# Expert weights in one run per partition, and fetched rows turned by 64x64 products

## The chip, the cores and the metric

One core of a Trainium2 chip runs the kernel alone. The metric is the device time of one execution in microseconds (us); the number that counts is the median of several executions.

## What is computed

The kernel is one encoder layer on 1024 tokens of 1024 channels with 16 meta tokens in front: a mixer (long convolutions and a gated recurrence), then a mixture of experts, then a norm. The change lies in the mixture of experts. Each token picks one of 8 groups and in it two of 8 experts, so two of 64 experts in all:

```python
def expert_block(args):
    xe, e = args
    return (jax.nn.silu(xe @ w_gate[e]) * (xe @ w_up[e])) @ w_down[e]
```

`w_gate[e]` and `w_up[e]` are 1024 x 512, `w_down[e]` is 512 x 1024, all float32, so each matrix has 2 MB and all 64 experts' matrices 403 MB. The outputs of a token's two experts are weighted and added to the residual.

## The kernel before

All 64 experts run one after the other, each on 64 slots for tokens (1024 tokens with two experts each fill 32 of 64 on average; slots beyond 64 of an expert are the business of `overflow`, behind a branch). The mixer and the router come first and end some 870 us after the start; they aren't touched by the change.

**Loads.** `expert_weights` (lines 1285 to 1306) loads one matrix, in the order gate, up, down of expert 0, then of expert 1, and so on, all on SP's queue. There are nine buffers, three experts' worth. Two things hold a load back: its buffer must have been used, and the load two before it must have landed (`AHEAD = 2`, a dependency that is added by hand), so that two loads are under way at any time. The first seven have their places early; the eighth and ninth (w_up and w_down of expert 2) wait for the rows of the first experts to be fetched. A matrix lies in SBUF as 128 partitions of 16 KB. Of w_down, partition p takes four rows of the matrix, which lie behind each other in memory: one run of 16 KB. Of w_gate and w_up, partition p takes rows 4p to 4p + 3 of the upper half of the matrix and the same of the lower half: two runs of 8 KB. The last w_up of all is loaded in two pieces of 1 MB, each with an instruction of its own, and only the second counts for the depth of the queue.

**Rows.** `fetch` gathers an expert's 64 rows of tokens by an indirect DMA from POOL: partition 64 h + s gets half h (512 channels and the norm's factor) of the row in slot s. Five buffers hold fetched rows. Slots without a token are left out of the transfer.

**One expert** (`expert`, lines 1321 to 1351). TensorE turns the rows: four transposes of 128x128 bring channels to partitions (`xt`), VectorE multiplies by the norm's gain into SBUF. Then sixteen products, alternating between w_gate and w_up, give `gu` in one PSUM bank, gate in partitions 0 to 63 and up in 64 to 127 (two column tiles of 64). ScalarE scales it into SBUF, four transposes (`ht`) turn it, ScalarE and VectorE apply silu and the product, and eight products with w_down give `y`. VectorE copies it out, and an indirect DMA from POOL scatters it to `yd` in DRAM. The `xt` tile in PSUM has one bank, in SBUF two buffers, so the rows of an expert are turned three experts ahead of their use.

**Order.** Each engine works in the order that a scheduler put down when the kernel was built; no table was written by hand. In the trace one product in float32 shows as two records of TensorE (and two weight loads), a transpose as one.

**After the experts**, `final` reads `yd`, adds, normalises and writes the output; it can begin when the last scatter has landed.

```python
    for j in range(4):
        nc.tensor.transpose(pt[:, j].rearrange("p h s -> p (h s)"), xg[:, j:512:4], e.ident)
...
    for i in range(8):
        h, j = divmod(i, 4)
        for z, w in enumerate((wg, wu)):
            nc.tensor.matmul(pg[64 * z:64 * z + 64], xt[:, j, h], w[:, h, j], start=i == 0, stop=i == 7)
```

## Time and profile before

| | |
|---|---|
| time, median of 3 runs | 1903.22 us (1899.13, 1903.22, 1906.44) |
| span of the profiled execution, first to last instruction | 1901.4 us |
| time of the profiled execution | not listed apart from the three runs; its span is 1.8 us below their median |
| mean granted TensorE clock, as a share of full speed | 0.963 |
| TensorE busy | 1627.3 us (86%) |
| TensorE weight loads | 979.9 us (52%) |
| VectorE, ScalarE, GpSimd busy | 817.9, 462.5, 184.5 us |
| moved by DMA | 574.54 MB, mean 302 GB/s |
| DMA busy, share of the 16 engines, in the 40 slices | 0.2 to 0.8 up to slice 17, then 0.9 or more to slice 38 |

The table has shares of the whole span, and the kernel has two parts with different limits. The experts fill slices 18 to 39 of the 40 (47.5 us each); what a change in them is worth must be read from those slices, from the waits of SP's queue and of TensorE there. A matmul's busy time runs to a modelled end and overlaps with that of its neighbours, so starts are a better guide than durations where many small products follow each other.

### The profile page before, as it was taken

The page shows a single profiled execution, that of the slowest core. Times are in us where ns is not written, and L with a number is a line of the kernel's source. Part 1 is how long each engine was busy: PE and PEld are TensorE (multiplying, and loading weights), DVE is VectorE, ACT ScalarE, POOL GpSimd, SP SyncE. Part 2 cuts the span into 40 slices and gives each one's busy share as a digit, 9 for nine tenths or more (in the row PEclk, how much of TensorE's full clock was granted, in tenths as well). Part 3 has the DMA queues.
Part 4 walks back from the last instruction along what each step waited for, and adds up shares of the span by engine and source line. Part 5 has one row for each costly group of instructions (what it writes and reads, how often), then busy time and mean ns, then how long its engine had stood idle before and what let it go on. Part 6 is the DMA issues. An engine that isn't in the chain of part 4 may idle for free. (4 is left out here: it accounts for less than half of the span.)

```text
span 1901.4 us, 22984 instructions
## 1 busy us (share of the span) xinstructions
PE 1627.3 (86%) x8907; PEld 979.9 (52%) x8907; DVE 817.9 (43%) x1661; ACT 462.5 (24%) x879; POOL 184.5 (10%) x223
## 2 busy tenths in 40 slices
PE   5999999999999798997998888888888888888882
PEld 3988988788787576883332223232222222222221
DVE  7678879687787987772111111111111111111106
ACT  5443345253436643331000000000000000000002
POOL 0011100000000001002111111111111111111000
PEclk7999999999999898998999999999999999999996
DMA  5365776566636437278999999999999999999987
GB/s 166 97 213 182 231 217 193 173 213 203 186 115 223 156 103 172 89 305 329 419 418 419 411 416 409 416 417 421 420 417 416 410 419 419 398 416 420 419 342 278
DMA packets 166887, 574.54 MB, mean 302 GB/s; under 512 B 20531, under 2 KB 85135, under 8 KB 125752
## 3 DMA queue, kind: packets, MB, share of 16 engines
q1 hardware_dynamic: 139816, 511.82, 68.6%
q0 software_dynamic: 25808, 57.00, 10.1%
q10 hardware_dynamic: 1152, 4.23, 0.5%
q8 instruction: 71, 1.16, 0.2%
q14 instruction: 40, 0.33, 0.1%
HBM read 532.79 MB, written 57.02 MB: 310 GB/s over the span
## 5 line engine op out<-in xcount | busy, mean ns | idle before, releaser
L1334 PE MATMUL gu<-w,xt 128*64 128x512 f32 x2048 | 517.1, 603 | 83.6 <-DMA w<-in_w_up 82.8
L1334 PEld LDWEIGHTS gu<-w,xt 128*64 128x64 f32 x2048 | 158.8, 138 | 425.8 <-issue 294.4
L1329 DVE TENSOR_TENSOR xt<-xt,gain 128x512 f32<-128x512 f32 x64 | 44.3, 692 | 535.0 <-PE gu L1334 497.0
L1347 PE MATMUL y<-w,ht 128*64 128x512 f32 x1024 | 238.3, 605 | 27.7 <-DVE ht L1342 27.7
L1336 ACT ACTIVATE gu<-gu,xg 128x512 f32<-128x512 f32 x64 | 44.0, 687 | 861.9 <-PE gu L1334 861.9
L480 PE MATMUL w<-al,wh 128*128 128x346 f32 (+2 forms) x672 | 235.1, 350 | 0.0
L480 PE MATMUL w<-ah,wh 128*128 128x346 f32 (+2 forms) x672 | 234.0, 349 | 0.7 <-ACT ah L232 0.7
L480 PE MATMUL w<-ah,wl 128*128 128x346 f32 (+2 forms) x672 | 233.6, 350 | 0.0
L1349 DVE COPY y<-y 128x512 f32<-128x512 f32 x64 | 44.3, 692 | 245.2 <-PE y L1347 245.2
L1347 PEld LDWEIGHTS y<-w,ht 128*64 128x64 f32 x1024 | 69.6, 138 | 153.9 <-issue 112.2
L480 PEld LDWEIGHTS w<-ah,wh 128*128 128x128 f32 x672 | 128.8, 192 | 10.9 <-issue 1.5
L480 PEld LDWEIGHTS w<-ah,wl 128*128 128x128 f32 x672 | 128.7, 192 | 10.8 <-issue 2.0
L480 PEld LDWEIGHTS w<-al,wh 128*128 128x128 f32 x672 | 128.8, 192 | 10.6 <-issue 1.6
L1315 POOL DMA_INDIRECT xg<-rdr,src x64 | 64.8, 1012 | 493.3 <-ACT gu L1336 483.5
L1350 POOL DMA_INDIRECT yd<-y,dst x64 | 64.9, 1014 | 374.7 <-DVE y L1349 374.7
L1339 PE MATMUL ht<-ident,gu 128*128 128x128 f32 x256 | 47.7, 309 | 49.9 <-ACT gu L1336 49.8
L1339 PEld LDWEIGHTS ht<-ident,gu 128*128 128x128 f32 x256 | 35.6, 208 | 102.8 <-ACT gu L1336 102.8
L1342 DVE TENSOR_TENSOR ht<-ht 128x256 f32<-128x256 f32 x64 | 26.9, 421 | 94.5 <-ACT ht L1341 92.5
L482 ACT ACTIVATE pc<-w 128x346 f32<-128x346 f32 (+2 forms) x84 | 41.8, 498 | 73.9 <-PE w L480 68.6
L470 ACT CAST wh<-w 128x512 fp32r<-128x512 f32 x64 | 39.6, 620 | 63.1 <-PE w L480 55.1
L446 PE MATMUL h<-fh,ftab 128*128 128x256 f32 x256 | 52.7, 287 | 2.2 <-ACT fh L433 2.0
L1327 PE MATMUL xt<-ident,xg 128*128 128x128 f32 x256 | 42.9, 290 | 11.4 <-DMA xg<-rdr,src 10.4
(421 smaller groups left out, 2255.4 us busy)
## 6 DMA issues: line engine op xcount, KB each, us to landing
w<-in_w_gate SPq DMA_DIRECT2D x64, 2048.0 KB
w<-in_w_down SPq DMA_DIRECT2D x64, 2048.0 KB
w<-in_w_up SPq DMA_DIRECT2D x63, 2048.0 KB
w<-in_w_in SPq DMA_DIRECT2D x64, 256.0 KB
ftab<-in_tab POOLq DMA_DIRECT2D x32, 384.0 KB, 4.2
tb<-in_tabf POOLq DMA_DIRECT2D x16, 768.0 KB, 6.1
ti<-in_tabi POOLq DMA_DIRECT2D x16, 640.0 KB, 5.4
kdr<-V SPq DMA_DIRECT2D x16, 512.0 KB
```

What stands on the lines that cost most here:

```text
L446: nc.tensor.matmul(A[-1][:, z * HC:z * HC + HC], lhs, rhs, start=i == 0, stop=i == len(prods) - 1)
L480: nc.tensor.matmul(pt[:, :n], lhs[k // 4][:, k % 4, :], rhs[:, k, c0:c0 + n], start=i == 0, stop=i == 3 * KT - 1)
L482: nc.scalar.activation(dst[:, c0:c0 + n], pt[:, :n], func)
L1315: d = nc.gpsimd.indirect_dma_start(out=xg, out_offset=None, in_=rows, in_offset=bass.IndirectOffsetOnAxis(ap=src, axis=0), bounds_check=2 ...
L1327: nc.tensor.transpose(pt[:, j].rearrange("p h s -> p (h s)"), xg[:, j:512:4], e.ident)
L1329: nc.vector.tensor_mul(xt, pt, gain[:, :, :, None].to_broadcast([P, 4, 2, SLOTS]))
L1334: nc.tensor.matmul(pg[64 * z:64 * z + 64], xt[:, j, h], w[:, h, j], start=i == 0, stop=i == 7)
L1336: nc.scalar.activation(gu, pg, AF.Copy, scale=xg[:, 512:513])
L1339: nc.tensor.transpose(pu[:, j].rearrange("p h s -> p (h s)"), gu[:, j::4], e.ident)
L1347: nc.tensor.matmul(py[64 * z:64 * z + 64], ht[:, j], wdv[:, j, z], start=j == 0, stop=j == 3)
L1349: nc.vector.tensor_copy(y, py)
L1350: nc.gpsimd.indirect_dma_start(out=ydv, out_offset=bass.IndirectOffsetOnAxis(ap=dst, axis=0), in_=y, in_offset=None, bounds_check=4 * SEQ ...
```

## The change

w_gate and w_up are laid out so that partition p takes rows 8p to 8p + 7 of the matrix: one run of 16 KB. Channel 8p + j then belongs to partition p. A row's half h holds channels 512 h to 512 h + 511, that is partitions 64 h to 64 h + 63, so the turned rows of half h must come out on these 64 partitions. The four 128x128 transposes become sixteen products of 64x64 (8 values of j, 2 halves) with the identity, at tile position (0, 0) for the first half and (64, 64) for the second. The turned tile has the same 512 columns as before, and the sixteen products with the weights stay as they were. The last w_up loses its two pieces and comes whole, as all others. All three matrices are loaded by one statement (line 1299 in the new file). The gain of the norm is loaded in the new layout. The comments are gone and lines move by one or two.

```diff
 def expert_weights(e, pools, i, after=None):
-    w = pools[i % 9].tile([P, 2, 4, 512], F32, name="w")
-    if j < 2:
-        src = I[("w_gate", "w_up")[j]][0, x].rearrange("(h p j) f -> p h j f", h=2, j=4)
-        if i == 3 * NE - 2:
-            nc.sync.dma_start(w[:, 0], src[:, 0])
-            d = nc.sync.dma_start(w[:, 1], src[:, 1])
-        else:
-            d = nc.sync.dma_start(w, src)
-    else:
-        d = nc.sync.dma_start(w.rearrange("p h j f -> p (h j f)"), I["w_down"][0, x].rearrange("(p j) c -> p (j c)", j=4))
+    w = pools[i % 9].tile([P, 8, 512], F32, name="w")
+    d = nc.sync.dma_start(w, weight_rows(I, ("w_gate", "w_up", "w_down")[j], x))
...
+def weight_rows(I, name, x):
+    m = I[name][0, x]
+    if name == "w_down":
+        return m.rearrange("(p j) (z c) -> p (j z) c", j=4, z=2)
+    return m.rearrange("(p j) f -> p j f", j=8)
...
 def expert(e, ps, xp, W, xg, dst, gain, ydv):
-    pt = ps.tile([P, 4, 2, SLOTS], F32, name="xt")
-    for j in range(4):
-        nc.tensor.transpose(pt[:, j].rearrange("p h s -> p (h s)"), xg[:, j:512:4], e.ident)
+    pt = ps.tile([P, 8, SLOTS], F32, name="xt")
+    for j in range(8):
+        for h in range(2):
+            r = slice(64 * h, 64 * h + 64)
+            nc.tensor.matmul(pt[r, j], xg[r, j:512:8], e.ident[r, r], start=True, stop=True, tile_position=(64 * h, 64 * h))
...
-            nc.tensor.matmul(pg[64 * z:64 * z + 64], xt[:, j, h], w[:, h, j], start=i == 0, stop=i == 7)
+            nc.tensor.matmul(pg[64 * z:64 * z + 64], xt[:, j], w[:, j], start=j == 0, stop=j == 7)
```

The scheduler puts the new products elsewhere than the transposes stood. This is TensorE's order for one expert x in the middle of the program, before; `gu` and `y` are the products with the weights, `ht` the transposes behind `gu`, and `xt` belongs to expert x + 3:

```order
L1334 MATMUL gu<-w,xt 64x512 x16
L1339 MATMUL ht<-ident,gu 128x128 x4
L1327 MATMUL xt<-ident,xg 128x128 x4
L1347 MATMUL y<-w,ht 64x512 x8
L1334 MATMUL gu<-w,xt 64x512 x16
```

The same place of the changed kernel:

```order
L1336 MATMUL gu<-w,xt 64x512 x15
L1341 MATMUL ht<-ident,gu 128x128 x4
L1330 MATMUL xt<-ident,xg 64x64 x14
L1348 MATMUL y<-w,ht 64x512 x8
L1336 MATMUL gu<-w,xt 64x512
L1330 MATMUL xt<-ident,xg 64x64 x2
L1336 MATMUL gu<-w,xt 64x512 x15
```

Fourteen of the sixteen new products stand where the four transposes stood, between `ht` and `y`; the last two have moved behind the next expert's first product with w_gate, ahead of its first product with w_up. The order is the same for all experts from about the tenth to the last that has rows to turn; in the first ten, eleven of the sixteen stand ahead of `ht`.

This is SP's queue at the last loads of weights, before:

```order
L1298 DMA w<-in_w_down 128x4096
L1296 DMA w<-in_w_gate 128x2x2048
L1293 DMA w<-in_w_up 128x2048
L1294 DMA w<-in_w_up 128x2048
L1298 DMA w<-in_w_down 128x4096
```

And of the changed kernel:

```order
L1299 DMA w<-in_w_down 128x4096
L1299 DMA w<-in_w_gate 128x4096
L1299 DMA w<-in_w_up 128x4096
L1299 DMA w<-in_w_down 128x4096
```

Every load of weights is now 128 pieces of 4096 numbers, where w_gate and w_up were 128 times two pieces of 2048, and the two half loads of the last w_up are one.

## Rows read from the trace of the kernel before

**Rows 1.** The page: span; DMA busy in 40 slices; GB/s in the same.

```profile
span 1901.4 us, 22984 instructions
...
DMA  5365776566636437278999999999999999999987
GB/s 166 97 213 182 231 217 193 173 213 203 186 115 223 156 103 172 89 305 329 419 418 419 411 416 409 416 417 421 420 417 416 410 419 419 398 416 420 419 342 278
```

**Rows 2.** Waits of SP's queue: total us, times, longest.

```profile
SPq L1296 <- DMA w<-in_w_up: 319.7, 63, 7.8
SPq L1298 <- DMA w<-in_w_gate: 292.2, 62, 8.9
SPq L1296 <- DMA w<-in_w_down: 287.7, 60, 5.7
```

**Rows 3.** Waits of all engines: TensorE's for weights.

```profile
PE gu L1334 <- DMA w<-in_w_up: 82.8, 49, 3.2
```

**Rows 4.** Timeline of SP's queue, three stretches: start us, us, issue.

```profile
1180.31 0.37 SPq L1296 DMA_DIRECT2D w<-in_w_gate  x1
1185.24 0.37 SPq L1296 DMA_DIRECT2D w<-in_w_up  x1
...
1300.90 0.34 SPq L1298 DMA_DIRECT2D w<-in_w_down  x1
...
1316.45 0.34 SPq L1298 DMA_DIRECT2D w<-in_w_down  x1
...
1795.51 0.37 SPq L1296 DMA_DIRECT2D w<-in_w_gate  x1
1800.77 0.37 SPq L1296 DMA_DIRECT2D w<-in_w_up  x1
1805.72 0.34 SPq L1298 DMA_DIRECT2D w<-in_w_down  x1
1810.69 0.37 SPq L1296 DMA_DIRECT2D w<-in_w_gate  x1
...
1825.85 0.37 SPq L1296 DMA_DIRECT2D w<-in_w_gate  x1
1826.27 0.46 SPq L1293 DMA_DIRECT2D w<-in_w_up  x1
1830.70 0.34 SPq L1294 DMA_DIRECT2D w<-in_w_up  x1
1836.05 0.33 SPq L1298 DMA_DIRECT2D w<-in_w_down  x1
```

**Rows 5.** Timeline of TensorE for one expert in the middle.

```profile
1314.14 0.75 PE L1339 MATMUL ht<-ident,gu 128*128 128x128 f32 x4 [0.83 <-ACT gu L1336]
...
1314.72 0.64 PE L1327 MATMUL xt<-ident,xg 128*128 128x128 f32 x4
...
1315.82 3.65 PE L1347 MATMUL y<-w,ht 128*64 128x512 f32 x16 [0.45 <-DVE ht L1342]
...
1319.30 1.02 PE L1334 MATMUL gu<-w,xt 128*64 128x512 f32 x2
...
1321.77 7.08 PE L1334 MATMUL gu<-w,xt 128*64 128x512 f32 x30 [1.45 <-DMA w<-in_w_up]
```

**Rows 6.** Timeline of TensorE in the recurrence: small float32 products in column tiles.

```profile
619.12 0.46 PE L936 MATMUL b<-lf,s 128*32 128x32 f32 x32
...
623.97 0.20 PE L936 MATMUL f<-qnb,s 128*32 128x32 f32 x1
624.10 0.27 PE L936 MATMUL f<-qff,kff 128*64 128x64 f32 x1
...
624.21 0.22 PE L936 MATMUL f<-qff,kff 128*64 128x64 f32 x1
```

**Rows 7.** Waits of SP's queue, 860 to 905 us.

```profile
SPq L1296 <- PE gu L1334: 1.4, 1, 1.4
```

**Rows 8.** Timeline of TensorE, the last expert.

```profile
1838.89 7.04 PE L1334 MATMUL gu<-w,xt 128*64 128x512 f32 x32
```

More of the change, by code (lines that the diff above doesn't have):

```diff
@@ L1324, in expert @@
     wg, wu, wd = W
-    pt = ps.tile([P, 4, 2, SLOTS], F32, name="xt")
-    for j in range(4):
-        nc.tensor.transpose(pt[:, j].rearrange("p h s -> p (h s)"), xg[:, j:512:4], e.ident)
-    xt = xp.tile([P, 4, 2, SLOTS], F32, name="xt")
-    nc.vector.tensor_mul(xt, pt, gain[:, :, :, None].to_broadcast([P, 4, 2, SLOTS]))
+    pt = ps.tile([P, 8, SLOTS], F32, name="xt")
[3 more added lines that the diff above has]
+            nc.tensor.matmul(pt[r, j], xg[r, j:512:8], e.ident[r, r], start=True, stop=True, tile_position=(64 * h, 64 * h))
+    xt = xp.tile([P, 8, SLOTS], F32, name="xt")
+    nc.vector.tensor_mul(xt, pt, gain[:, :, None].to_broadcast([P, 8, SLOTS]))
     pg = ps.tile([P, 512], F32, name="gu")
-    for i in range(8):
-        h, j = divmod(i, 4)
+    for j in range(8):
         for z, w in enumerate((wg, wu)):
-            nc.tensor.matmul(pg[64 * z:64 * z + 64], xt[:, j, h], w[:, h, j], start=i == 0, stop=i == 7)
+            nc.tensor.matmul(pg[64 * z:64 * z + 64], xt[:, j], w[:, j], start=j == 0, stop=j == 7)
     gu = xp.tile([P, 512], F32, name="gu")
@@ L1342, in expert @@
     nc.vector.tensor_mul(ht, ht, pu[:, :, 1])
-    wdv = wd.rearrange("p h j f -> p (h j f)").rearrange("p (j z c) -> p j z c", j=4, z=2)
     py = ps.tile([P, 512], F32, name="y")
@@ L1346, in expert @@
         for z in range(2):
-            nc.tensor.matmul(py[64 * z:64 * z + 64], ht[:, j], wdv[:, j, z], start=j == 0, stop=j == 3)
+            nc.tensor.matmul(py[64 * z:64 * z + 64], ht[:, j], wd[:, 2 * j + z], start=j == 0, stop=j == 3)
     y = xp.tile([P, 512], F32, name="y", bufs=3)
@@ L1423, in overflow @@
             for j, name in enumerate(("w_gate", "w_up", "w_down")):
-                w = op.tile([P, 2, 4, 512], F32, name=f"ow{j}")
+                w = op.tile([P, 8, 512], F32, name=f"ow{j}")
                 src = I[name][0, bass.ds(x, 1)].rearrange("e a b -> (e a) b")
                 if j < 2:
-                    nc.sync.dma_start(w, src.rearrange("(h p j) f -> p h j f", h=2, j=4))
+                    src = src.rearrange("(p j) f -> p j f", j=8)
                 else:
-                    nc.sync.dma_start(w.rearrange("p h j f -> p (h j f)"), src.rearrange("(p j) c -> p (j c)", j=4))
+                    src = src.rearrange("(p j) (z c) -> p (j z) c", j=4, z=2)
+                nc.sync.dma_start(w, src)
                 W.append(w)
@@ L1668, in build @@
         last = [w_out_load(e, wc, (6, 7), cs, f"l{i}") for i, cs in enumerate(columns(512))]
-        gain = kp.tile([P, 2, 4], F32, name="gain")
-        nc.sync.dma_start(gain, I["norm_ffn"].rearrange("o (h p j) -> p (o h) j", h=2, j=4))
-        gain = gain.rearrange("p h j -> p j h")
+        gain = kp.tile([P, 8], F32, name="gain")
+        nc.sync.dma_start(gain, I["norm_ffn"].rearrange("o (p j) -> (o p) j", j=8))
         for tt in range(8):
```

## The prediction

> **What bounds the kernel now.** I read the page first, and in it the slices. From slice 18 on the DMA engines are busy at 0.9 or more and move 398 to 421 GB/s, and before it they are far from that [rows 1]. So the experts' part is the place, and what counts there is how fast the weights come. The waits of SP's queue say the same from the other side: nearly every load is issued at the moment when the load two before it lands, 319.7 + 292.2 + 287.7 us of waiting on loads in all [rows 2]. The reader is to see that the queue never waits for a buffer: loads wait for loads. TensorE then waits for what comes late, w_up, 82.8 us in 49 times, 1.29 us for each of the 64 experts [rows 3].
>
> Because a load is issued when the one two before it lands, the times of issue in SP's timeline are times of landing, and the distance of two of them is what one load took of the engines' time. One expert goes from 1300.90 to 1316.45, so 15.55 us for three matrices [rows 4]. TensorE's timeline of the same expert shows the slack: behind the first product with w_gate (1319.30) it waits until 1321.77, and 1.45 us of that is the wait for w_up [rows 5]. So the loads set the pace, and TensorE is about a tenth faster.
>
> **The change, part by part.**
>
> *The runs of 16 KB.* The trace already holds loads with such runs: w_down. In the last experts no rows are fetched any more and the landings are clean. From the issue of w_up at 1800.77 to that of w_down at 1805.72 landed a w_gate: 4.95 us. From there to 1810.69 landed a w_up: 4.97 us. From 1795.51 to 1800.77 landed a w_down, 5.26 us, but with the scatter of an expert's output among it. A w_down without that stands elsewhere: 1180.31 to 1185.24, 4.93 us [rows 4]. So 2 MB in runs of 16 KB take 4.93 us and in runs of 8 KB 4.95 to 4.97 us; the gain is 0.02 us for a w_gate and 0.04 for a w_up, and I take 0.02 for each. 123 loads of w_gate and w_up lie on the path: those of experts 3 to 63 and the w_up of expert 2, which is the first that waits for the rows. The term is 123 x 0.02 = 2.5 us less. Its bounds: nothing at all, if 0.02 is chance; and the shortest w_down that I find, from 1825.85 to 1830.70, 4.85 us [rows 4], which is 0.10 below a w_gate, so 12.3 us less. I take the 4.93, since the 4.85 comes from the place where the half loads disturb the queue. A loss I exclude, since w_down has been loaded in just this way all along.
>
> *The last w_up.* It came in halves, the first issued at 1826.27 right behind the last w_gate and ahead of its turn, the second at 1830.70. Thanks to that, the last expert's sixteen products began at 1838.89, as soon as TensorE was free, and ended 7.04 us later at 1845.93 [rows 4, 8]. Now w_up is issued whole at 1830.70. The last w_gate lands at 1836.05 (that is when the last w_down was issued), and w_up lands 4.97 us later, at 1841.02. From there the remaining products take 7.08 us, as they do for any other expert that waits for w_up [rows 5], so they end at 1848.10: 2.2 us more. Behind them lies the chain to the last scatter, and then the final norm, with nothing beside it; this term is on the path in full. The last w_down lands 4.93 us behind w_up, at 1845.95, before those products end, and holds nothing up.
>
> *Sixteen products for four transposes.* Between `ht` and `y` there was room for the transposes: they began at 1314.72, and `y` at 1315.82 waited for VectorE, so 1.10 us are free there [rows 5]. Now fourteen products stand in that room, and two in the wait for w_up. The trace before has no 64x64 product with both tile positions, so I bound its price. The nearest row is the recurrence's product of 128x64 with 64 columns, two of them abreast in two column tiles: its second record starts 0.11 us behind its first (624.10, 624.21) [rows 6]. A product has two records, so a pair abreast costs 0.21 us. That is a pair alone, however; the run of 32 records with 32 columns in four column tiles takes 0.46 us, of which 0.20 is the length of the last, so 0.26 us over 7 steps, 0.037 us a step for 32 columns, and twice that for 64: 0.15 us for a pair [rows 6]. I take 0.15, as the run is long like ours. Each change of tile size costs 0.13 us from start to start (623.97 to 624.10) [rows 6]. With a price p for a pair, `y` moves back by 0.13 + 7p + 0.13 - 1.10, and the two late products with their two changes cost p + 0.26, together 8p - 0.58: 0.62 us for each expert at p = 0.15, 1.10 at 0.21. Both are under the 1.29 us that TensorE has to spare for each expert [rows 3], so the term is nothing. What hides it is the wait for w_up; without it, it would cost 64 x 0.62 = 40 us.
>
> *The first expert.* Sixteen products instead of four transposes stand ahead of its first product with weights: 8p is 1.2 to 1.7 us against 0.64 [rows 5, 6], up to 1.0 us later. There SP did wait for TensorE once, 1.4 us [rows 7], so a later expert 0 delays one load. As the queue holds two, the other is still under way then; I take nothing, and keep 1.0 us for the range. Loads, VectorE's product with the gain and the gain's own load cost the same as before, as the tile keeps its 512 columns.
>
> **Sum.** -2.5 + 2.2 + 0 + 0 = -0.3 us. The profile has a span of 1901.4 us [rows 1] and the median of three runs is 1903.22, 1.8 above it; what lies around the span isn't touched, so the sum is made on the median: 1902.9 us, no change that a measurement can tell from none. For that I take 0.5%, 9.5 us.
>
> **Rivals.** *Slower: the products run one after another.* The two tiles of a pair share no rows and no columns of the array, but they write the same PSUM bank, and no row here shows two row tiles at work together; the pairs in rows 6 are column tiles that read the same 128 rows. If a pair costs twice, p = 0.30, each expert costs 8 x 0.30 - 0.58 = 1.82 us, 0.53 more than the slack of 1.29, and TensorE becomes the bound: 64 x 0.53 = 34 us, 1937 us; with 0.42 it is 2.78 - 1.29 = 1.49 us each and 1998 us (the other terms drop out, as the loads are then no longer last). It decides from p = 0.234 on. Against it: half of p = 0.30 is already scaled up, and 8 pairs would have to reach 1.9 us. I give it 0.12. The Trainium skill speaks for it: TensorEngine Tiling (Array Packing), Gotcha 1: PSUM Pressure, says that different row tiles cannot access the same PSUM bank at the same time, and its Key Properties say that a change of tiling mode drains the engine. The 0.13 us at each change agree with the second; the first no row here shows.
>
> *Faster: the short gap counts.* If the 4.85 us of one w_down are what 16 KB runs really take, and the other w_downs are longer because scatters and fetches mix with them, then 62 x 0.10 + 61 x 0.12 = 13.5 us go and 2.2 come back: 1891.9 us. It decides, against the 9.5 us, from 0.095 us for each load on. For it speaks that one row; against it, the 4.93 us of a w_down that nothing disturbed. I give it 0.09. The Trainium skill, DMA: Bandwidth & Descriptors, section Where 436 GB/s comes from, puts the ceiling at 435.2 GB/s; by that a load of 2 MB could not take less than an estimated 4.82 us. The 4.95 us of a w_gate are 424 GB/s, so the trace agrees that little is left.
>
> That the change doesn't do what it says I exclude: in the order of SP's queue every load of weights is 128 pieces of 4096 numbers.
>
> **Numbers.** The forecast has 0.79, the slower rival 0.12, the faster 0.09, and as their bounds are the 9.5 us, these are the chances of same, slower and faster. The range goes down to the faster rival with a little for the spread of runs, 1891, and up to 1903.2 + 2.2 + 1.0 and the 3.2 us by which the highest run lies above the median, 1910. It leaves out the slower rival and little else.
>
> **What would show it.** Right: SP's queue still waits on loads alone; landings without fetch and scatter stand 4.93 us apart for all three matrices, and 15.5 us for an expert; the wait for w_up is still there, shorter by 0.5 to 1 us each; in the last expert TensorE waits some 2 us for w_up. Pairs of the new products start 0.15 to 0.21 us apart. Wrong, slower: the wait for w_up is gone, SP waits for TensorE's products, and an expert takes 16 us or more. Wrong, faster: an expert takes 15.3 us or less.

## The result, and the profile after

The changed kernel takes 1919.38 us (median of four runs, 1910.32 to 1922.04) against 1903.86 us before: 1.0079 of the time before, 95% interval 1.0057 to 1.0101. Measured again later beside other kernels (e16 below) it was 1.0056 (1.0040 to 1.0073). So it is slower, by 0.6 to 0.8%, where I had forecast no change. The profiled run is the fastest of the four, 1910.32 us with a span of 1908.6, so its profile shows less of the loss than the median does.

The page after: the span, busy time by engine, and in 40 slices DMA and GB/s, to be read beside [rows 1].

```profile
span 1908.6 us, 26570 instructions
...
PE 1742.6 (91%) x10699; PEld 1092.9 (57%) x10699; DVE 817.6 (43%) x1661; ACT 462.7 (24%) x879; POOL 184.6 (10%) x223
...
DMA  5366776576626437378999999999999999999957
GB/s 171 93 210 198 227 211 188 179 221 196 186 100 233 145 112 161 141 281 348 424 391 409 424 417 424 422 422 421 420 418 410 414 424 417 412 421 424 418 236 277
```

The DMA engines are as full as before in the experts' part, but slice 38, counted from 0, has fallen from 342 to 236 GB/s: the loads are done, and something else is still at work. TensorE's busy time has grown to 1742.6 us (1627.3 before).

The waits after: SP's queue, the lines that answer to [rows 2], then SP's wait for TensorE, and then the two largest waits of TensorE within the experts (total us, times, longest).

```profile
SPq L1299 <- DMA w<-in_w_gate: 311.1, 62, 7.2
SPq L1299 <- DMA w<-in_w_up: 297.4, 63, 7.4
SPq L1299 <- DMA w<-in_w_down: 283.6, 61, 6.2
...
SPq L1299 <- PE gu L1336: 14.2, 10, 5.0
...
PE ht L1341 <- ACT gu L1338: 47.2, 57, 0.9
PE gu L1336 <- DVE xt L1332: 5.5, 7, 0.8
```

SP still waits for loads above all, but it now waits for TensorE too: 14.2 us in 10 times for products with w_gate and w_up, whose buffer the next load needs, most of it ahead of 1010 us. And the line of [rows 3], TensorE waiting 82.8 us for w_up, isn't there any more: TensorE never waits for weights. It has become the last in the chain. These are two of the three signs that the prediction named for its slower rival; the third, 16 us or more for an expert, is there only now and then, as the following shows.

The timeline of TensorE for one expert in the middle, beside [rows 5]: start us, duration, and what it waited for.

```profile
1318.36 0.75 PE L1341 MATMUL ht<-ident,gu 128*128 128x128 f32 x4 [0.83 <-ACT gu L1338]
1319.03 1.90 PE L1330 MATMUL xt<-ident,xg 64*64 64x64 f32 x28
1320.86 3.65 PE L1348 MATMUL y<-w,ht 128*64 128x512 f32 x16
1324.34 1.02 PE L1336 MATMUL gu<-w,xt 128*64 128x512 f32 x2
1325.29 0.46 PE L1330 MATMUL xt<-ident,xg 64*64 64x64 f32 x4
1325.68 7.08 PE L1336 MATMUL gu<-w,xt 128*64 128x512 f32 x30
1333.59 0.75 PE L1341 MATMUL ht<-ident,gu 128*128 128x128 f32 x4 [0.83 <-ACT gu L1338]
```

From `ht` to `ht` it is 15.23 us with nothing but ScalarE's copy to wait for.

A good clock for the whole stretch is ScalarE's copy of `gu`, one for each expert. The first and the last of the 64, before and then after:

```profile
880.34 0.69 ACT L1336 ACTIVATE gu<-gu,xg 128x512 f32<-128x512 f32 x1 [16.82 <-PE gu L1334]
...
1846.05 0.69 ACT L1336 ACTIVATE gu<-gu,xg 128x512 f32<-128x512 f32 x1 [11.15 <-PE gu L1334]
```

```profile
879.21 0.69 ACT L1338 ACTIVATE gu<-gu,xg 128x512 f32<-128x512 f32 x1 [18.29 <-PE gu L1336]
...
1856.56 0.69 ACT L1338 ACTIVATE gu<-gu,xg 128x512 f32<-128x512 f32 x1 [11.15 <-PE gu L1336]
```

The next copies before start at 892.37, 904.57, 916.77, 928.97, 944.62, 957.68 ...; after at 893.51, 908.30, 924.64, 939.40, 955.55, 973.03 .... From the first to the last of the 64 it is 965.71 us before (880.34 to 1846.05) and 977.35 after (879.21 to 1856.56), 11.6 more. I call this **the stretch** below. It is steadier than the total: what comes ahead of it differs from run to run (in two profiles of one kernel, e1 and e15, the first copy came at 878.45 and at 887.06). In these two profiles the spans differ by only 7.2 us, since after begins 1.1 us sooner and has 52.0 us behind its last copy where before has 55.4. The kernel before was profiled once, so how far its own stretch varies isn't shown; after and e16 differ by 0.04 us, e1 and e15 by 1.1.

The rest shows in the products with w_down. Four windows after, the second with products of w_gate and w_up, the others with a `y`: from, to, length, busy time of the five engines (with the number of instructions), granted clock, DMA share, GB/s.

```profile
1195.60:1200.70 5.10, 5.10 (x18) 1.56 (x17) 0.00 (x0) 0.00 (x0) 0.00 (x0) 0.67 1.02 424
1202.20:1209.00 6.80, 6.80 (x30) 2.08 (x30) 0.00 (x0) 0.00 (x0) 0.76 (x1) 1.00 0.99 415
1212.60:1217.60 5.00, 5.00 (x16) 1.50 (x17) 0.00 (x0) 0.00 (x0) 0.00 (x0) 0.66 1.01 421
1229.50:1232.80 3.30, 3.30 (x18) 1.14 (x17) 0.00 (x0) 0.00 (x0) 0.00 (x0) 1.00 1.00 419
```

In the first and third the granted clock is 0.67 and 0.66, so most of the time at the lower of the two levels, 1.2 GHz, and the `y` of these experts takes 5.3 us; in the last it is full and `y` takes 3.65. Ahead of each stand a wait of 0.83 us for ScalarE, four transposes and fourteen small products. From the ninth expert on, those with such a fall take 16.9 us and the others 15.23. Twelve `y` in all fall so, four of them in the first nine experts. The kernel before has four falls between its first and last copy, all behind the point from which TensorE waits for w_up.

### The profile page after: what moved, and what is told of

The parts are those of the page before. It is cut to its first block, busy times and chain, and to the rows that moved or that the text cites. A ratio compares the mean times of both kernels' runs of the same rounds, so it can differ in the third digit from the quotient of the medians.

```text
span 1908.6 us, 26570 instructions
## 1 busy us (share of the span) xinstructions
PE 1742.6 (91%) x10699; PEld 1092.9 (57%) x10699; DVE 817.6 (43%) x1661; ACT 462.7 (24%) x879; POOL 184.6 (10%) x223
## 5 line engine op out<-in xcount | busy, mean ns | idle before, releaser
L1336 PEld LDWEIGHTS gu<-w,xt 128*64 128x64 f32 x2048 | 164.7, 137 | 295.3 <-issue 280.4
L1348 PE MATMUL y<-w,ht 128*64 128x512 f32 x1024 | 256.9, 638 | 2.8 <-DVE ht L1344 2.8
L1330 PEld LDWEIGHTS xt<-ident,xg 64*64 64x64 f32 x2048 | 134.9, 211 | 71.1 <-issue 59.6
L1330 PE MATMUL xt<-ident,xg 64*64 64x64 f32 x2048 | 152.5, 287 | 11.3 <-DMA xg<-rdr,src 10.5
L1348 PEld LDWEIGHTS y<-w,ht 128*64 128x64 f32 x1024 | 75.8, 145 | 131.5 <-issue 122.8
```

The lines of the kernel that those rows point to most:

```text
L1330: nc.tensor.matmul(pt[r, j], xg[r, j:512:8], e.ident[r, r], start=True, stop=True, tile_position=(64 * h, 64 * h))
L1336: nc.tensor.matmul(pg[64 * z:64 * z + 64], xt[:, j], w[:, j], start=j == 0, stop=j == 7)
L1348: nc.tensor.matmul(py[64 * z:64 * z + 64], ht[:, j], wd[:, 2 * j + z], start=j == 0, stop=j == 3)
```

## The experiments

Three theories. **T**: TensorE became the bound, through the products' time, the split pair (two of them between an expert's first product with w_gate and its partner with w_up) and the falls of its clock. **L**: the loads in runs of 16 KB are slower. **W**: the last w_up in one piece costs it. The diffs show only the lines that matter; "..." marks what is left out between them. The table is their summary; each ratio is to runs of the kernel before on the same chip; "expert" is the usual distance of two copies where TensorE is behind the loads and its clock is full (in e5 the clock falls in every expert). e1, e2 and e15 pair the channels of rows and weights otherwise than the reference; the others compute it.

| kernel | median us | ratio to before (95%) | stretch us | expert us |
|---|---|---|---|---|
| before | 1901 to 1904 | | 965.71 | 13.06 |
| after / e16 | 1919.38 / 1911.81 | 1.0079 / 1.0056 | 977.35 / 977.31 | 15.23 |
| e1 / e15 loads alone | 1892.03 / 1891.54 | 0.9953 (0.9936 to 0.9969) / 0.9948 (0.9935 to 0.9961) | 957.07 / 958.21 | 13.06 |
| e2 products alone | 1910.66 | 1.0053 (1.0035 to 1.0072) | 977.39 | 15.23 |
| e3 sixteen in one place | 1900.53 | 1.0002 (0.9983 to 1.0020) | 962.79 | 14.12 |
| e4 eight of 128 columns | 1896.18 | 0.9983 (0.9965 to 1.0001) | 955.86 | 13.4 to 14.2 |
| e5 one half, then the other | 2012.03 | 1.0572 (1.0536 to 1.0608) | 1068.24 | 17.07 |
| e6 pairs of full rows | 1903.60 | 1.0006 (0.9987 to 1.0025) | 959.64 | 13.98 |
| e7 eight in one place | 1901.15 | 0.9994 (0.9975 to 1.0014) | 957.12 | 13.05 |
| e8 split pair, before | 1903.60 | 0.9992 (0.9970 to 1.0013) | 963.87 | 14.70 |
| e9 eight and eight | 1901.71 | 1.0011 (0.9997 to 1.0025) | 961.74 | 13.34 |
| e10 filled wait | 1896.44 | 0.9977 (0.9960 to 0.9994) | 962.60 | 15.23 |
| e11 / e12 rows stored | 1917.50 / 1918.30 | 1.0088 / 1.0081 | 972.54 / 975.18 | 13.06 |
| e13 loads in order | 1913.37 | 1.0060 (1.0047 to 1.0074) | 972.96 | 13.06 |
| e14 eight and eight, halves | 1897.69 | 0.9980 (0.9961 to 0.9998) | 958.73 | 13.34 |
| e17 / e18 rows beside | 1909.44 / 1904.41 | 1.0067 / 1.0019 | 956.30 / 956.84 | 13.06 |

### e1 and e2: each half of the change by itself

```diff
 e1, on the kernel before
-        src = I[("w_gate", "w_up")[j]][0, x].rearrange("(h p j) f -> p h j f", h=2, j=4)
+        src = I[("w_gate", "w_up")[j]][0, x].rearrange("(p h j) f -> p h j f", h=2, j=4)
 e2, on the changed kernel
+        src = I[("w_gate", "w_up")[j]][0, x].rearrange("(h p j) f -> p h j f", h=2, j=4)
...
+        if i == 3 * NE - 2:
+            nc.sync.dma_start(v[:, 0], src[:, 0])
+            d = nc.sync.dma_start(v[:, 1], src[:, 1])
```

> The kernel before with one thing of the change: w_gate and w_up come in runs of 16 KB (the last w_up still in two halves, the four transposes kept). Channels of the rows and of the weights are then paired differently from the reference; no instruction of TensorE differs from before. Theory T (TensorE became the last in the chain; the loads are not to blame): TensorE waits for w_up for some 80 us as in [rows 3], an expert takes about 15.5 us in the steady part, 1899 to 1906 us. Rival L (loads in runs of 16 KB land later): 1913 to 1922 us, with longer waits for w_up.

> The changed kernel with the loads of before (w_gate and w_up in two runs of 8 KB, the last w_up in two halves): of the change only the sixteen products are left. Channels of the rows and of the weights are paired differently from the reference. Theory T: the wait of TensorE for w_up (82.8 us before) is gone, an expert takes 14 to 19 us in the first eight and 15.2 or 16.9 after, 1912 to 1922 us. Rival L (the loads): 1900 to 1906 us with the wait for w_up still there. Rival W (the last w_up whole costs it): 1906 to 1912 us.

The loads alone make the kernel *faster*, by 0.47% of the time, under what either theory had expected; the products alone make it slower, with the stretch of the changed kernel to 0.04 us. By its time alone, 1910.66, e2 lies just under the range of T and in that of W, so it is the trace that decides: the last w_up is in halves there, and the stretch is all the same. L and W fall, T stands. In e1 the wait of [rows 3] is still there, and in e2 TensorE's largest wait within the experts is that of the changed kernel:

```profile
PE gu L1334 <- DMA w<-in_w_up: 74.9, 48, 2.7
```

```profile
PE ht L1350 <- ACT gu L1347: 47.2, 57, 0.9
```

Against e1 the change thus misses a gain of about 9 us in the stretch, since TensorE is last, and loses some 12 us on top.

### e3: sixteen in one place

```diff
         nc.tensor.transpose(pu[:, j].rearrange("p h s -> p (h s)"), gu[:, j::4], e.ident)
+    if nxt is not None:
+        pt, last = turn(e, ps, nxt)
...
+            if last and (j, z) == (0, 0):
+                e.tc.add_manual_dep(m.ins, last.name,
...
```

(`turn` issues the sixteen products of a later expert; the dependency holds the first product of `y` behind the last of them.)

> The changed kernel with its sixteen products in one place: all sixteen between the transposes of the gated rows and the products with w_down, so that no pair of gate and up products is split; nothing is added or left out. Theory T says that a split pair costs TensorE 0.95 + 0.39 - 0.47 - 0.26 = about 0.6 us an expert: the expert falls from 15.2 to about 14.6 us at the full clock, TensorE catches up with the loads and waits for w_up again, 1902 to 1910 us. Rival P (the products' own time is all of it, their place nothing): the expert stays at 15.2 us, no wait for w_up, 1914 to 1922 us.

The time falls to that of before, 1.0002 (1900.53 us, just under the range of T). Same products, same number, another place. TensorE's timeline of e3, one expert while it is behind the loads:

```profile
1004.01 7.04 PE L1344 MATMUL gu<-w,xt 128*64 128x512 f32 x32
1011.91 0.75 PE L1351 MATMUL ht<-ident,gu 128*128 128x128 f32 x4 [0.86 <-ACT gu L1348]
1012.59 2.14 PE L1327 MATMUL xt<-ident,xg 64*64 64x64 f32 x32
1014.66 3.65 PE L1360 MATMUL y<-w,ht 128*64 128x512 f32 x16
```

Sixteen products take 2.07 us (1012.59 to 1014.66), 0.129 each and 0.26 a pair. An expert is 14.12 us. Against 15.23 that is 1.11 for the split alone, nearly twice what I expected of it: all sixteen products of gate and up take 7.04 us, and the fifteen that are left behind a split take 7.08, so the lone one comes on top with its 0.95 us. Against before's 13.06 it is 1.06 for the products' own time. From the twentieth expert on TensorE waits for w_up again.

### e4 and e7: eight products of 128 columns

```diff
+    for i in range(4):
+        for q in range(2):
+            nc.tensor.matmul(pt[64 * q:64 * q + 64, i].rearrange("p h s -> p (h s)"), xg[:, 2 * i + q:512:8], e.ident, start=True, stop=True)
...
+    for h in range(2):
+        for q in range(2):
+            o, r = slice(64 * h, 64 * h + 64), slice(64 * q, 64 * q + 64)
+            nc.vector.tensor_mul(xt[o, :, q], pt[r, :, h], gain[r, h, :, None].to_broadcast([64, 4, SLOTS]))
 e7 also
+            if last and (j, z) == (0, 0):
+                order(e, m.ins, last)
```

(`order` holds an instruction behind another of the same engine, as the dependency in e3 does; here `y` behind the last of the eight.)

> The runs of 16 KB with another way of turning: eight products of 128 rows by 64 columns of the fetched rows with the 128 x 128 identity, pairs of them into the two halves of the partitions, then four multiplications on VectorE instead of one, which put each quarter on its partitions; the last w_up in two halves as before. It computes the reference. Theory T: four pairs cost at most 4 x 0.23 = 0.9 us where four transposes cost 0.58, so TensorE has at most 0.4 us more than before for an expert and waits for w_up in the steady part; the loads set the end, 1897 to 1905 us. Rival L: 1911 us or more whatever TensorE does. Rival P2 (a pair of 128 columns costs twice a pair of 64, and VectorE's four smaller multiplications come late): 1910 to 1920 us.

> The kernel of e4_eight_of_128_columns with its eight products in one place, between the transposes of the gated rows and the products with w_down; it computes the reference. There an expert took 13.4 to 14.2 us while TensorE was behind; with no split pair 12.7 to 13.2 us, TensorE catches up within seven experts instead of fifteen. The end is set by the loads in both: 1890 to 1900 us, not to be told from e4 by the time alone; if TensorE still sets part of it, some 3 us less than e4.

Both compute the reference with the loads of the change, and their stretches, 955.86 and 957.12 us, are those of the loads alone. Eight such products take 1.08 us in e7 and its expert is 13.05 us, the same as with four transposes before:

```profile
952.40 1.25 PE L1331 MATMUL xt<-ident,xg 128*64 128x128 f32 x16
953.48 3.61 PE L1369 MATMUL y<-w,ht 128*64 128x512 f32 x16
```

By the time, e4 is at 0.9983 and e7 at 0.9994; e7's first copy came at 885.79 and e4's at 880.63, which is the uneven part ahead of the stretch. So the place of the eight made no difference to the stretch, as expected where the loads are last; by the median e4 came out just below its range and e7 1 us above. In e7, as in e8, e9 and e14, the rows are turned two experts ahead and not three, which wasn't tried by itself.

### e5 and e6: do two products run abreast?

```diff
 e5, on e3
-    for j in range(8):
-        for h in range(2):
+    for h in range(2):
+        for j in range(8):
 e6, on e3
-            m = e.nc.tensor.matmul(pt[r, j], xg[r, j:512:8], e.ident[r, r], start=True, stop=True, tile_position=(64 * h, 64 * h))
+            m = e.nc.tensor.matmul(pt[r, j], xg[:, j:512:8], e.ident[:, r], start=True, stop=True)
```

> The kernel of e3_sixteen_in_one_place with the two loops over the products exchanged: eight products of the upper half of the partitions, then eight of the lower, so that two neighbours are never on different halves. Nothing is left out. If two products of a pair ran abreast (my prediction's step 3), sixteen in a row take up to twice their 2.07 us, about 4 us, the expert 16 us, TensorE never catches up, 1920 to 1935 us. If they run one after another anyway (the rival of the prediction), 2.1 us again, and 1896 to 1904 us as e3.

> The kernel of e3_sixteen_in_one_place with products of 128 rows by 64 columns: both products of a pair take all 128 partitions of the fetched rows and half the columns of the 128 x 128 identity; shapes of the outputs, their number and their place are as in e3, the rows of the array are no longer split. It computes the reference. If the split of the rows (and going in and out of it) is what makes sixteen products 2.07 us, they take 1.0 to 1.6 us and the expert 13.1 to 13.7 before TensorE catches up. If it is a fixed price for each product (its load of 64 columns), 2.0 to 2.2 us again. In both cases the loads set the end, 1894 to 1904 us.

TensorE's timeline of e5 and then of e6, from the small products to `y`:

```profile
1405.58 3.68 PE L1327 MATMUL xt<-ident,xg 64*64 64x64 f32 x32
1409.19 5.05 PE L1360 MATMUL y<-w,ht 128*64 128x512 f32 x16
```

```profile
951.32 2.15 PE L1327 MATMUL xt<-ident,xg 128*64 128x64 f32 x32
953.29 3.60 PE L1360 MATMUL y<-w,ht 128*64 128x512 f32 x16
```

Without alternation the sixteen take 3.61 us instead of 2.07, so the pairs did run abreast: the rival of the prediction had the wrong mechanism. The single records say the same: in e3 the two of a pair start within 0.01 us of each other and the next two 0.12 us later, in e5 each one starts some 0.12 us behind the one before. This isn't the clock, which falls only near the end of e5's sixteen: up to 1407.40 it is granted in full. With full rows they take 1.97, so the split of the rows costs next to nothing; a pair of 64 columns costs 0.25 to 0.26 us in either shape, as the second expectation for e6 had it. The Trainium skill, TensorEngine Tiling (Array Packing), Gotcha 1: PSUM Pressure, has it that different row tiles cannot use one PSUM bank at the same time; the 2.07 against 3.61 us, all in one bank, do not look like that. e5 went further up than I expected, 2012 us: 17.07 us an expert, and `y` takes 5.05 us in every one, a fall of the clock each time.

### e8: the split in the kernel before

```diff
+            if (i, z) == (0, 0) and nxt is not None:
+                pt, last = turn(e, ps, nxt, m.ins)
+            if (i, z) == (0, 1) and last:
+                order(e, m.ins, last)
```

(`turn` is here the four transposes, of the expert two ahead, held behind the first product; its partner is held behind them.)

> The kernel before with only the place of the four transposes changed: they stand between the first product with w_gate and its partner with w_up, as two of the sixteen did in the changed kernel; nothing is left out. Theory T (a split pair costs about 1.1 us, here with some 0.6 more because the transposes no longer fill the wait for the gated rows): an expert takes 13.6 to 14.2 us instead of 12.2 while TensorE is behind, TensorE catches up around the twentieth expert, later falls are hidden in the wait for w_up, which shrinks from 82.8 to under 30 us; 1900 to 1908 us. Rival P (the place costs nothing): 12.2 us an expert at first, a wait of some 80 us.

TensorE never waits for w_up here either, not even as a rest of 30 us, and yet the time stays, 0.9992. An expert takes 14.70 us and every second one 16.39, whose `y` takes 5.35:

```profile
1404.53 0.74 PE L1360 MATMUL ht<-ident,gu 128*128 128x128 f32 x4 [0.83 <-ACT gu L1357]
1406.20 5.35 PE L1368 MATMUL y<-w,ht 128*64 128x512 f32 x16 [0.93 <-DVE ht L1363]
1411.39 1.02 PE L1350 MATMUL gu<-w,xt 128*64 128x512 f32 x2
1412.34 0.75 PE L1329 MATMUL xt<-ident,xg 128*128 128x128 f32 x4
```

The mean of the two is the loads' 15.55 [rows 4]: TensorE gains on the loads only slowly and is level with them at the end, 10.45 us from the last issue of w_down to the last copy. The split costs what T says (13.06 + 1.1, and 0.5 for the bare wait for `ht`, make 14.7), though I had worked out 13.6 to 14.2. What I had not foreseen is that the falls come at nearly every second expert, thirty in all.

### e9 and e14: eight and eight

```diff
+        last = turn(e, pt, nxt, range(4), m.ins)
...
+        last = turn(e, pt, nxt, range(4, 8), m.ins)
 e14 also
+    if i == 3 * NE - 2:
+        nc.sync.dma_start(w[:, :4], src[:, :4])
+        d = nc.sync.dma_start(w[:, 4:], src[:, 4:])
```

> The changed kernel, computing the reference, with the sixteen products in two places: eight behind the products of gate and up, where TensorE waits about 0.85 us for ScalarE's copy, and eight between the transposes of the gated rows and the products with w_down, where it waits for the gated rows; no pair of gate and up products is split. With 0.129 us a product: 7.04 + 1.03 + 0.67 + 1.03 + 3.48 and little waiting, about 13.3 us an expert instead of 15.23 (after) and 14.12 (e3). Theory T: TensorE catches up within about nine experts, waits for w_up again for 50 us or more, and the loads in runs of 16 KB set the end: 1891 to 1900 us, the whole change a gain. Rival: the products cost more beside other work, 1900 us or more.

> The kernel of e9_eight_and_eight with the last w_up in two halves, as before the change; it computes the reference. From the last landing to the copy of the last gate and up products: 10.0 us instead of 12.1 (step 2 of my prediction, 2.2 us). By the loads 1892 to 1900 us; against e9's 1901.7 a fall of 2.1 us if nothing else moves.

An expert takes 13.34 us as worked out, TensorE catches up at the thirteenth, waits 56.7 us for w_up and hardly for ScalarE any more (1.7 us). The time of e9 was nevertheless 1.0011, above what I expected; e14 brings 0.9980. One part of the difference is step 2 of the prediction. The last load is issued when the last w_gate has landed; from there to the last copy it is 12.14 us in e9 (1829.26 to 1841.40), 12.16 in e3 and 12.17 in e10, with w_up whole, and 10.01 in e14 and 10.00 before, in halves (9.99 to 10.57 in most others with halves, 11.8 in e13 and e15, where the clock falls at the last `y` but one). SP's timeline of e14, its last issue, and ScalarE's, its last copy of `gu`:

```profile
1833.78 0.33 SPq L1304 DMA_DIRECT2D w<-in_w_down  x1
```

```profile
1843.79 0.69 ACT L1367 ACTIVATE gu<-gu,xg 128x512 f32<-128x512 f32 x1 [11.15 <-PE gu L1361]
```

So 2.15 us, as forecast (2.2), where the loads are last. In the changed kernel it is nothing, as TensorE is late anyway.

### e10: filling the wait

```diff
+    pf = ps.tile([P, 512], F32, name="fill")
+    for j in range(4):
+        f = nc.tensor.transpose(pf[:, 128 * j:128 * j + 128], e.ident, e.ident)
+        if j == 0:
+            order(e, f.ins, m.ins)
```

> The changed kernel with four transposes of the identity added for each expert, into a bank of PSUM that nothing reads, behind the products of gate and up, where TensorE is idle for 0.8 us while ScalarE copies; the order of everything else stays, split pair included. Theory T on the clock: the falls of the granted clock at the products with w_down (5.3 instead of 3.65 us, nine to ten times) come with this idle stretch and the small products behind it; with it filled they vanish or become fewer, every expert takes 15.2 to 15.3 us, and the time falls by up to 16 us from the changed kernel's, to 1898 to 1908 us. Rival: the falls have nothing to do with the stretch, 1910 to 1922 us with 16.9 us about every tenth expert; or the four transposes outlast the wait and every expert takes longer.

Four useless transposes for each expert make the changed kernel faster: 0.9977 of before, where the changed kernel stands at 1.0056 to 1.0079. From the eighth distance of copies to the fifty-third each expert takes 15.23 to 15.26 us, none 16.9:

```profile
1402.84 0.66 PE L1346 MATMUL fill<-ident 128*128 128x128 f32 x4
1403.73 0.75 PE L1351 MATMUL ht<-ident,gu 128*128 128x128 f32 x4 [0.24 <-ACT gu L1343]
1404.41 1.90 PE L1335 MATMUL xt<-ident,xg 64*64 64x64 f32 x28
1406.23 3.65 PE L1360 MATMUL y<-w,ht 128*64 128x512 f32 x16
```

And the windows of e10, two of 100 us, with a granted clock of 1.00, as everywhere between its first and last copy:

```profile
1000.00:1100.00 100.00, 98.31 (x572) 42.83 (x568) 11.52 (x19) 7.33 (x14) 13.50 (x14) 1.00 1.01 418
1400.00:1500.00 100.00, 98.32 (x588) 43.93 (x586) 11.94 (x20) 7.50 (x14) 13.19 (x13) 1.00 1.01 417
```

That shows the third cause apart from the others, since from the eighth expert on the products and the split pair are as in the changed kernel. Its stretch is 962.60, 14.7 us shorter, but not all of that is the clock. In the first experts the order differs too: in the changed kernel `y` of the first six stands mixed with the next expert's `gu`, in e10 only that of the first, and the first eight distances add up to 122.0 us against 128.6. From the ninth copy on, where the order is the same, e10 is 8.2 us shorter. There nine falls, up to 1.7 us each, are gone, 15 us; part of that isn't seen, because in the last ten experts TensorE has caught up and waits for w_up again, 3.3 us in all.

### e11 to e13, e17, e18: the same loads with four transposes, computing the reference

Is the gain of e1 that of the loads, although e1 pairs the channels otherwise? To keep the four transposes, the normed rows were stored in another order of channels, by a copy before the store.

```diff
+    o = rp.tile([P, 2, ROW], F32, name="ro")
+    for h in range(2):
+        (nc.vector.tensor_copy if h else nc.scalar.copy)(
+            o[:, :, 256 * h:256 * h + 256].rearrange("p g (m i) -> p m g i", i=4),
+            hres[:, tt, h, :512].rearrange("p (m g i) -> p m g i", g=2, i=4))
...
+    d = nc.scalar.dma_start(rows[tt * P:tt * P + P], o)
 e13 also
+    if e.wdma:
+        order(e, d.ins, e.wdma[-1])
 e17 also
+    o = rp.tile([P, 2, ROW], F32, name="ro", bufs=1)
```

e12 is e11 with the last w_up whole; e18 is e17 with two buffers, into which the square of the rows is written first.

> The runs of 16 KB with the four transposes of before, made to compute the reference by the order in which the normed rows are stored: groups of four channels in turn to the two halves of a row, by one copy of each half tile on ScalarE and VectorE before the store (8 tiles of tokens; the last one, about 0.7 us later, lies ahead of the first fetch). Products of gate and up are held behind the products with w_down from the sixth expert on. The last w_up comes in halves. TensorE as before, loads as in e1_loads_alone: 1890 to 1896 us, the wait for w_up about 75 us. If the copies come late for the first rows, up to 5 us more.

> The kernel of e11_rows_stored_for_the_runs with the last w_up in one transfer instead of two halves; it computes the reference. My prediction's step 2: with the loads last, TensorE's last products of gate and up start after the whole of it and the end comes 2.2 us later, 1892 to 1898 us; by the time alone that is hardly to be told, by the trace it is: the wait for the last w_up and the distance from the last landing to the end of those products. If the products start on time anyway, no difference.

> The kernel of e11_rows_stored_for_the_runs with each load of weights held behind the one before it on SP, so that they come expert by expert as in the kernel before; in e11 the order of the queue had come out as two w_up, two w_gate, two w_down of neighbouring experts, and experts took 13.06 and some 18 us in turn. It computes the reference; four transposes, runs of 16 KB, the last w_up in halves. If the runs of 16 KB are worth the 8.6 us that e1_loads_alone showed: 1890 to 1896 us, an expert about 15.4 us with a wait for w_up of some 75 us. If e1 was fast for another reason (its data, its chip): 1899 to 1904 us.

> The kernel of e13_loads_in_order with the copy of the rows in another place of the memory, one buffer instead of two, where it overlaps none of the first seven matrices: in e13 it lay on the place of one of them, the first nine loads came late (72 GB/s instead of about 300 in slice 18 of the page) and the first products of gate and up with them. It computes the reference. If the gain of e1 is that of the runs of 16 KB: 1890 to 1897 us, 0.995 to 0.998 of before, slice 18 near 300 GB/s, the first copy of gate and up products before 888 us. If it is 1900 us or more with the loads on time, e1's gain is not that of its loads.

> As e17_rows_beside_old_place, with two buffers for the copied rows (the square of the rows is written into them first), so that the copy of a tile does not wait for the store of the tile before it, but VectorE's half waits for the square of its own tile, about 1 us. It computes the reference. Same bounds as e17; within 2 us of it.

All five missed, each for a reason that the trace shows. In e11 and e12 SP's order had changed, two w_up in a row, two w_gate, two w_down, so that an expert's third matrix came late, and experts took 13.06 and some 18 us in turn; whether the last w_up is whole couldn't be seen in that. In e13 the copied rows lay on the place of an early matrix, and its third load was issued at 872.03 instead of 806.07 (e1), and at 808.12 in e17, where the rows lie elsewhere. In e17 the first seven came on time, but the eighth, which waits for the rows, at 887.39 instead of 868.10. SP's timeline of e17, then of e1:

```profile
839.52 0.33 SPq L1302 DMA_DIRECT2D w<-in_w_gate  x1
887.39 0.34 SPq L1302 DMA_DIRECT2D w<-in_w_up  x1
```

```profile
837.73 0.33 SPq L1296 DMA_DIRECT2D w<-in_w_gate  x1
868.10 0.34 SPq L1296 DMA_DIRECT2D w<-in_w_up  x1
```

Counted from the first load of weights, the eighth came 87.05 us later in e17 and 81.33 in e18, against 69.92 in e1, 69.94 before and 70.04 in e15. So the copies, for which I had reckoned 0.7 us, held the rows back by 11 to 17 us: in e17 a copy waits for the store of the tile before (1.30, 0.74 and 2.69 us for the last three). But the stretch, which begins with the first expert, answers the question: 956.30 and 956.84 us in e17 and e18, 957.07 and 958.21 in e1 and e15, 965.71 before. The gain of the loads, 7.5 to 9.4 us, is there with right results as well.

### e15 and e16: e1 and the change again

> The kernel of e1_loads_alone once more, beside e13 and e14 on the same chip (channels of rows and weights paired differently from the reference, nothing else). If its gain belongs to the runs of 16 KB: 0.993 to 0.997 of before again, and e13 within 3 us of it. If it belonged to that chip or hour: 0.999 or more.

> The changed kernel once more, beside the others on the same chip: 1.006 to 1.010 of before if its loss is its own (TensorE last to the end, falls of the clock at the products with w_down); 1.000 to 1.004 if part of it belonged to the chip of the first comparison.

e15 repeats the gain of e1, 0.9948, though e13 didn't come near it, for the reason above. e16 has the stretch of the first comparison, 977.31, and lies a little below its expected range by the ratio, 1.0056; its loss is its own.

## Why the prediction was wrong

**The runs of 16 KB** (step 1, -2.5 us, bounds 0 and -12.3): right in sign, too small. The stretch alone moves by -8.6 and -7.5 us. From 900 to 1800 us the median w_gate went from 5.00 us (before) to 4.92 (e1) and the median w_up from 5.35 to 5.28, 0.07 to 0.08 each, and 123 of those are 9 us. I had taken 0.02 us a load, from a w_down of 4.93 us without a scatter among it. But that landing, 1180.31 to 1185.24, wasn't undisturbed: POOL issued a scatter at 1180.69, and 50 packets of its queue lie within. POOL's timeline, and the DMA queues of that window (packets, MB, share):

```profile
1180.69 1.02 POOL L1350 DMA_INDIRECT yd<-y,dst  x1 [5.12 <-DVE y L1349]
```

```profile
q1 hardware_dynamic: 166, 1.88, 94.3%
q0 software_dynamic: 50, 0.04, 2.5%
```

The 4.85 us that I set aside has no packet of that queue. Most landings of w_gate have none either, or next to none, and their median is 4.99 us before (47 of them) and 4.92 in e1 (43): the 0.07 is there without any disturbance.

**The last w_up** (step 2, +2.2): 2.15 measured where the loads are last, nothing in the changed kernel.

**Sixteen products for four transposes** (step 3, 0, "both are under the 1.29 us that TensorE has to spare"): this is the step that failed, in three ways.

First its price, 0.62 us an expert. A pair costs 0.26, not 0.15: the step of 0.037 us from 32-column products with four abreast [rows 6] doesn't carry over to 64 columns with two. The other row that I had, 0.21 for a pair alone, was nearer. By itself the sixteen make 1.06 us (14.12 - 13.06), and e3 shows that this would have been hidden. The split pair I priced as one pair and two changes, 0.41; it costs 1.11, because fifteen products take as long as sixteen. I could have read that in [rows 5]: there too a lone first product takes its 1.02 and the other fifteen 7.08, against 7.04 for all [rows 8]. It was free there only because w_up was late. Together 2.17 us.

Then the slack. 1.29 us was the wait for w_up, averaged. What TensorE had to spare in the steady part was the loads' 15.55 less its own 13.06, 2.49 us: in [rows 5] the 1.45 us of waiting and the 1.02 of the lone product ahead of it, which costs nothing only while the engine waits. So even 2.17 fit, with 0.3 left (0.4 to 0.5 by the mean of the loads over the middle, 15.6 to 15.7). But TensorE begins late. Before, the first eight experts came at 12 to 13 us (one at 15.65) and made good 15.55 x 8 - 103.5 = 20.9 us of arrears; that is what the wait for w_up, 49 times and not 64, says. After, the first eight take 14.3 to 19.6, 128.6 us in all; in e3 they take 116.0, so about half of what is lost there goes with the order, which I had not priced. The arrears can be measured: from the landing of an expert's w_up to its copy, less the 7.1 us of its products, the twelfth expert before has none, and after it is 24.3 us late, the last but one still 14.5. In e3 it is 13.1 and gone by the twentieth, in e10 19.2 and gone by the fifty-fifth. At 0.3 to 0.5 us an expert 24.3 us last nearly to the end.

Then the falls of the clock at `y`, up to 1.7 us twelve times, nine of them from the ninth copy on, which use up most of what this small lead wins. The prediction doesn't speak of them. They cost time only where TensorE is last: e3 has thirteen and is level with before, where one fall makes a distance of 17.95 us and the next 13.85. e10, without any and with another order in its first experts, ends 0.2% below the time before.

**The first expert** (step 4, 0): nothing speaks against it; the first copy comes at 879.21, before at 880.34, but with 8.6 us between two profiles of one kernel (e1, e15) a term of 1 us couldn't be seen there.

**The rivals.** The slower one named the outcome, TensorE last and no wait for w_up, by the wrong mechanism, and the loss was about half of its 34 us: pairs do run abreast (e5), and its point of decision, p = 0.234, falls with the slack of 1.29, as e3 has p = 0.26 and loses nothing. The faster one was near the truth for the loads alone (e1 1892.03, its 1891.9 for another sum; that the two agree so closely is luck), but didn't come to pass.

Two slips in the prediction change nothing: counted from 0, slice 18 has 0.8 and 329 GB/s, and 0.9 begins with slice 19; and in the faster rival the 61 and the 62 loads are exchanged, 13.5 us either way.

## What to carry to other kernels

A mean wait is not slack: compare each engine's own period with the bound's, and ask how far behind it starts and how many rounds it has to catch up. Where small work is put between two products that run as a pair, the pair's time is paid nearly twice, and an order that is free while the engine waits is not free once it is the bound. Look at both halves of a change by themselves: here one gained 0.5%, and of that the whole change keeps 0.2%, and only in another order (e14) or with the idle time filled (e10).

## What I had not expected of the hardware

- Useless work made the kernel faster: four transposes in a wait of 0.83 us held the granted clock at 1.00, and the median fell from 1911.81 or 1919.38 to 1896.44 us (e10; part of it by another order in the first experts).
- How often the granted clock falls goes with what fills the time ahead of `y`. Between the first and the last copy it is never in e10, nor in e4; twelve times with a wait of 0.83 us and fourteen 64x64 products (after); thirteen times with a wait of 0.86 us and sixteen (e3); thirty times where TensorE waits a further 0.93 us (e8); at every expert that has rows to turn with the sixteen that don't alternate (e5). Only the filled wait was tried by itself.
- Two 64x64 float32 products on different rows and columns take 0.26 us as a pair and 0.45 on the same ones; a pair with all 128 rows takes 0.25. A pair of 128 columns (e7, 1.08 us for four) takes 0.27, hardly more than one of 64.
- 2 MB in runs of 16 KB instead of 8 save 0.07 to 0.08 us, 4.92 against 4.99 where next to nothing of the fetches and scatters mixes in. Why they save it wasn't tried.
